# Layer 0's attention with the two query halves in the two row halves of TensorE's array

## The chip, the cores and the metric

The kernel runs on one core of a Trainium2 chip. The metric is the device time of one execution in microseconds (us). The engines are TensorE (PE; its weight loads are shown as PEld), VectorE (DVE), ScalarE (ACT), GpSimd (POOL) and SyncE (SP, which issues the DMAs). The numbers are float32; most matmuls read their operands as fp32r, those of the probabilities with the values as plain f32.

## The reference, cut to what matters

Two layers follow each other over 1024 latent tokens and 256 context tokens. Layer 0 is grouped-query attention with 16 heads of 64 numbers and 4 groups, layer 1 latent attention with 16 heads. The change is in layer 0's attention:

```python
def gqa_attend(q, k, v):
    s = jnp.einsum('bqhgd,bkhd->bhgqk', q, k).astype(jnp.float32) * (GQA_HEAD_DIM ** -0.5)
    p = jax.nn.softmax(s, axis=-1).astype(v.dtype)
    return jnp.einsum('bhgqk,bkhd->bqhgd', p, v)
```

Latent queries read all 1280 keys, context queries the 256 context keys. Queries and keys are normed and rotated before.

## The kernel before, in words

**Order of the work.** Layer 0's projections come first (to about 275 us of the profile), then gate slices for layer 0 (`gate_slice`, to 368 us; the first row maxima stand among them), layer 0's attention (368 to 765 us), its output projection with layer 1's projections, layer 1's attention (1197 to 1642 us) and the last output projection.

**Split numbers.** Every query and key is kept as a rounded number and a rest (QH and QL, KH and KL), since an fp32r product rounds its operands. A score is KH·QH + KL·QH + KH·QL, less a shift, which is the largest product of the query's row. Layer 0 has heads of 64 numbers, so before the change a tile KA holds KH in rows 0 to 63 and KL in rows 64 to 127, QA holds QH twice, KB holds KH with a row of -1 below it (65 rows), and QB holds QL with the row of shifts `crow` below it. KA·QA and KB·QB are then all of it, in two steps (`l0_scores`, L1141).

**Units.** The class `Attention` works through units. A latent unit is one head with its 1024 queries and ten tiles of 128 keys; a context unit is one group's four heads with 256 queries each and two key tiles. There are 16 latent and 4 context units in layer 0. For each key tile `do_scores` (L413) issues two steps for each of the two query halves of 512 (four matmuls at L422) into a score tile `st` of two PSUM banks, of which there are two, and ACT makes the probabilities `p` of it (L424). After the unit's tiles, `do_av` (L458) multiplies the probabilities by the values: the outputs of the two query halves lie in PSUM partitions 0 to 63 and 64 to 127, each step 128 rows by 64 columns.

**Maxima.** The row maxima of units to come are made between the score steps: a matmul of 128 queries by 512 keys into a PSUM tile `mx` (L362; for the context keys two of 256, L367), which DVE then reduces (L363, L369). A latent unit needs 20 of them, a context unit 4; `do_scores` puts two into each key tile, in front of the first and of the third matmul, and `maxima` lets them run 28 ahead. There are two `mx` buffers. When a unit's maxima are there, DVE takes the largest (L376), PE turns them (L382, "turn"), DVE copies (L384) and a DMA writes the row `crow`.

**Sums.** POOL adds up the first six probability tiles (L445), DVE the last four in pairs (L431). One unit later PE folds the sum over the partitions with four 32-column steps (`total`, L500), into the old `av` tile; DVE transposes it and takes reciprocals (L504, L505). Then POOL scales the output (L519, L520).

**What sets the order.** In `run` the orders of PE, DVE and ACT are written out by hand (`manual_schedule`): the unit's key tiles, the turn, the total of the unit before, then `do_av`. In the gate slices before 368 us a scheduler places the maxima, four after each gate slice (L1171 and on, `at.maxima(at.done + 4, 2)`). POOL's and SP's orders are the scheduler's everywhere.

## Time and profile before

| what | value |
|---|---|
| time, median of 3 runs (lowest, highest) | 1738.92 us (1737.24, 1739.38) |
| profiled execution, first to last instruction | 1736.6 us |
| layer 0's attention in it | 368 to 765 us |
| granted TensorE clock, mean | 0.997 |
| HBM read and written | 158.98 and 73.63 MB |

The profiled execution is told by its span; the three timed runs lie 0.6 to 2.8 us above that span, with what lies around the instructions. A row of the timeline gives the start, the time to the end of the last instruction of the row, engine, line, names, and the number of merged instructions. A matmul's own duration contains a latency, so the pace is read from the distance of two starts. PEld is the load of the stationary operand that belongs to each matmul.

### The profile page before, as it was taken

The page shows a single profiled execution, that of the slowest core. Times are in us where ns is not written, and L with a number is a line of the kernel's source. Part 1 is how long each engine was busy: PE and PEld are TensorE (multiplying, and loading weights), DVE is VectorE, ACT ScalarE, POOL GpSimd, SP SyncE. Part 2 cuts the span into 40 slices and gives each one's busy share as a digit, 9 for nine tenths or more (in the row PEclk, how much of TensorE's full clock was granted, in tenths as well). Part 3 has the DMA queues.
Part 4 walks back from the last instruction along what each step waited for, and adds up shares of the span by engine and source line. Part 5 has one row for each costly group of instructions (what it writes and reads, how often), then busy time and mean ns, then how long its engine had stood idle before and what let it go on. Part 6 is the DMA issues. An engine that isn't in the chain of part 4 may idle for free. (4 is left out here: it accounts for less than half of the span.)

```text
span 1736.6 us, 23794 instructions
## 1 busy us (share of the span) xinstructions
PE 1703.1 (98%) x8548; PEld 1232.5 (71%) x8548; DVE 1068.4 (62%) x1807; ACT 644.5 (37%) x943; POOL 979.5 (56%) x657
## 2 busy tenths in 40 slices
PE   8999999999999999999989999999999999999998
PEld 5776778776655665558878798978666666657587
DVE  3765651368777877625575667756676767667231
ACT  4632221134544544433244633332343443434310
POOL 2763430237888897752344644443587878777511
PEclk9999999999999999999999999999999999999999
DMA  9457854432332422156434857685434443441452
GB/s 326 156 160 235 265 167 136 133 98 55 100 91 71 116 66 74 44 145 189 137 94 132 238 163 199 181 234 162 104 88 118 108 104 91 111 112 43 118 162 73
DMA packets 211901, 234.33 MB, mean 135 GB/s; under 512 B 20680, under 2 KB 157880, under 8 KB 211784
## 3 DMA queue, kind: packets, MB, share of 16 engines
q1 hardware_dynamic: 211360, 232.71, 47.2%
q8 instruction: 67, 1.10, 0.3%
q14 instruction: 50, 0.41, 0.1%
q10 hardware_dynamic: 424, 0.11, 0.0%
HBM read 158.98 MB, written 73.63 MB: 134 GB/s over the span
## 5 line engine op out<-in xcount | busy, mean ns | idle before, releaser
L363 DVE TENSOR_REDUCE m<-mx 128x1 f32<-128x512 f32 x512 | 351.5, 691 | 203.6 <-PE mx L362 201.5
L424 ACT ACTIVATE p<-st 128x1024 f32<-128x1024 f32 x328 | 335.3, 1024 | 219.5 <-PE st L422 185.1
L445 POOL TENSOR_TENSOR acp<-acp,p 128x1024 f32<-128x1024 f32 x128 | 305.7, 2388 | 8.7
L458 PE MATMUL av<-p,v 128*64 128x512 f32 x1312 | 289.9, 595 | 0.0
L458 PEld LDWEIGHTS av<-p,v 128*64 128x64 f32 x1312 | 90.8, 137 | 181.0 <-issue 178.6
L445 POOL TENSOR_TENSOR acp<-p 128x1024 f32<-128x1024 f32 x34 | 81.3, 2391 | 168.3 <-ACT p L424 167.9
L445 POOL TENSOR_TENSOR acp<-acp,acd 128x1024 f32<-128x1024 f32 x60 | 141.5, 2358 | 22.2 <-DVE acd L431 19.4
L431 DVE TENSOR_REDUCE acd<-p 128x512 f32<-128x1024 f32 x124 | 144.6, 1219 | 7.7 <-ACT p L424 7.7
L135 POOL TENSOR_TENSOR wb<-wraw,wa 128x512 fp32r<-128x512 f32 (+3 forms) x73 | 95.5, 1324 | 90.6 <-ACT wa L156 90.0
L92 PE MATMUL mm<-wa,hh 128*128 128x512 f32 (+2 forms) x336 | 127.3, 379 | 1.7 <-ACT hh L787 1.7
L422 PE MATMUL st<-QH,KL 96*128 96x512 f32 x320 | 123.5, 392 | 0.0
L94 PE MATMUL mm<-wa,hl 128*128 128x512 f32 (+2 forms) x336 | 121.3, 361 | 1.4 <-DVE hl L790 1.4
L93 PE MATMUL mm<-wb,hh 128*128 128x512 f32 (+2 forms) x336 | 120.9, 360 | 0.0
L479 ACT COPY os<-av 128x512 f32<-128x512 f32 x36 | 21.1, 586 | 252.9 <-PE av L458 173.5
L369 DVE TENSOR_REDUCE m<-mx 128x2 f32<-128x512 f32 x144 | 99.3, 692 | 25.3 <-PE mx L367 24.4
L92 PE MATMUL y<-wa,oh 128*128 128x512 f32 (+1 forms) x296 | 114.1, 386 | 0.0
L93 PE MATMUL y<-wb,oh 128*128 128x512 f32 (+1 forms) x296 | 113.6, 384 | 0.0
L94 PE MATMUL y<-wa,ol 128*128 128x512 f32 (+1 forms) x296 | 113.6, 384 | 0.0
L422 PE MATMUL st<-QA,KA 128*128 128x512 f32 x336 | 106.6, 399 | 0.7 <-ACT p L424 0.7
L422 PE MATMUL st<-QB,KB 65*128 65x512 f32 x336 | 105.5, 395 | 0.0
L362 PE MATMUL mx<-KA,QA 128*128 128x512 f32 x256 | 102.4, 405 | 1.2 <-DVE m L363 1.0
L362 PE MATMUL mx<-KH,QH 96*128 96x512 f32 x256 | 102.3, 401 | 0.0
(232 smaller groups left out, 3423.4 us busy)
## 6 DMA issues: line engine op xcount, KB each, us to landing
mraw<-in_l_w_mod SPq DMA_DIRECT2D x64, 256.0 KB
wraw<-in_l_w_in SPq DMA_DIRECT2D x28, 512.0 KB
rb<-rrow SPq DMA_DIRECT2D x72, 128.0 KB
mraw<-in_l_w_mod SPq DMA_DIRECT2D x16, 512.0 KB
sgd<-gth SPq DMA_DIRECT2D x32, 256.0 KB
QA<-q0h SPq DMA_DIRECT2D x32, 256.0 KB
wraw<-in_l_w_out SPq DMA_DIRECT2D x16, 512.0 KB
sg<-sgd SPq DMA_DIRECT2D x64, 128.0 KB
```

The source lines that it names most:

```text
L92: pe.matmul(ps, lhsT=lh(k), rhs=rh(k), start=first and i == 0, stop=False)
L93: pe.matmul(ps, lhsT=lh(k), rhs=rl(k), start=False, stop=False)
L94: pe.matmul(ps, lhsT=ll(k), rhs=rh(k), start=False, stop=last and i == len(ks) - 1)
L135: eng.tensor_sub(lo, a, b)
L362: pe.matmul(m, lhsT=s["mq"][:, i * P:(i + 1) * P], rhs=s["mk"][:, n * 512:(n + 1) * 512], start=True, stop=True)
L363: dve.reduce_max(s["m"][:, i, n:n + 1], m, axis=AX.X)
L369: dve.reduce_max(s["m"][:, 2 * i:2 * i + 2, 2 if u["kind"] == "lat" else 0], m.rearrange("p (a b) -> p a b", a=2), axis=AX.X)
L422: pe.matmul(ps[:, n * 512:(n + 1) * 512], lhsT=lh, rhs=rf(n), start=(j == 0), stop=(j == len(prods) - 1))
L424: act.activation(p, ps, AF.Exp, scale=self.ops["scale"])
L431: dve.reduce_sum(t[:, ns], p2.rearrange("p a n -> p n a")[:, ns, :], axis=AX.X)
L445: pool.tensor_add(t, a, b)
L458: pe.matmul(s["av"][64 * n:64 * n + 64, :], lhsT=s["v"][:, kt, u["vc"]:u["vc"] + 64], rhs=p[:, n * 512:(n + 1) * 512], start=kt == kts[0], ...
```

## The change

In layer 0 alone (`HALVES = (True, False)`; the functions for layer 1 are there, but not called) each query half gets its own 64 rows of the array: QH and QL are tiles of 128 rows by 512, with the first query half in rows 0 to 63 and the second in rows 64 to 127; KA holds KH in both row halves, KB holds KL in both. A score is then four steps of 64 rows for each half: KH·QH, KL·QH, KH·QL, and a step that subtracts the shift, in which the stationary tile `minus` has -1 in rows 0 and 64 and a tile `shift` the shifts in the same rows (zeros elsewhere, written once). `scores_by_halves` writes the steps of the two halves alternately. A maximum is one product of 64 rows with KH and QH alone; two are made per key tile, one in each row half, the second put after two of the other half's steps. The `mx` tiles go from two to three, the `av` tiles from two to one, and the total goes to an `mx` tile. The row of shifts is written by two DMAs in place of one, from one buffer in place of two. The diff, cut to layer 0:

```diff
+HALVES = (True, False)
...
-            self.ps_m = st.enter_context(tc.tile_pool(name=f"psm{l}", bufs=2, space=PSUM, side="right", reuse_waits="tile"))
+            self.ps_m = st.enter_context(tc.tile_pool(name=f"psm{l}", bufs=3 if HALVES[l] else 2, space=PSUM, side="right", reuse_waits="tile"))
+            if HALVES[l]:
+                self.ops["open"](self, st)
...
-                setattr(self, name, stp.enter_context(tc.tile_pool(name=f"{name}{l}", bufs=2, space=PSUM, reuse_waits="tile")))
+                bufs = 1 if HALVES[l] and name == "ps_o" else 2
+                setattr(self, name, stp.enter_context(tc.tile_pool(name=f"{name}{l}", bufs=bufs, space=PSUM, reuse_waits="tile")))
...
+        def max_parts(self, u, step):
+
+            s = self.state[id(u)]
+            kind, i, n = step
+            if kind == "lat":
+                half, spans = i // 4, [(i % 4, slice(n * 512, n * 512 + 512), slice(0, 512))]
+            else:
+                half, spans = i // 2, [(2 * (i % 2) + a, slice(NL, NT), slice(a * 256, a * 256 + 256)) for a in range(2)]
+            held = {}
...
+            def part(j):
+                if j == 0:
+                    held["m"] = self.ps_m.tile([P, 512], F32, name="mx", tag="mx")
+                pairs = self.ops["maxima"](s, half)
+                q, k = pairs[j]
+                for t, ks, cs in spans:
+                    pe.matmul(held["m"][:, cs], lhsT=q[:, t * P:(t + 1) * P], rhs=k[:, ks], start=j == 0, stop=j == len(pairs) - 1)
+                if j == len(pairs) - 1:
+                    dve.reduce_max(s["m"][:, i, n:n + 1], held["m"], axis=AX.X)
...
-                r = self.sm.tile([8, P], F32R, name="crow", tag="crow", bufs=2)
+                r = self.sm.tile([8, P], F32R, name="crow", tag="crow", bufs=1)
                 dve.tensor_copy(r, t)
-                sp.dma_start(raw(s["crow"]), raw(r))
+                if HALVES[self.l]:
+                    for n in range(2):
+                        sp.dma_start(raw(s["crow"][n]), raw(r[4 * n:4 * n + 4, :]))
+                else:
+                    sp.dma_start(raw(s["crow"]), raw(r))
...
+            if HALVES[self.l]:
+                if lat:
+                    self.todo += [(u, ("lat", i + 4 * a, n)) for i in range(4) for n in range(2) for a in range(2)]
+                self.todo += [(u, ("ctx", i + 2 * a, 0)) for i in range(2) for a in range(2)]
...
+        @staticmethod
+        def side_by_side(*streams):
+
+            for t in range(max(map(len, streams))):
+                for stream in streams:
+                    if t < len(stream):
+                        stream[t]()
...
+        def scores_by_halves(self, u, kt, p, steps):
+
+            s = self.state[id(u)]
+            ps = self.ps_s.tile([P, 1024], F32, name="st", tag="st")
+            prods = [self.ops["scores"](s, kt, n) for n in range(2)]
+            last = len(prods[0]) - 1
...
+            streams = [[lambda j=j, n=n: product(j, n) for j in range(last + 1)] for n in range(2)]
+            for half, parts in steps:
+                at_ = (last + 2) // 2 if half else 0
+                streams[half][at_:at_] = parts
+            self.side_by_side(*streams)
+            act.activation(p, ps, AF.Exp, scale=self.ops["scale"])
...
-                t = s["av"] if u is not self.units[-1] else self.ps_m.tile([P, 512], F32, name="mx", tag="mx")
+                t = s["av"] if u is not self.units[-1] and not HALVES[l] else self.ps_m.tile([P, 512], F32, name="mx", tag="mx")
...
-                            self.do_scores(u, kt, ps[i], one_more)
+                            if HALVES[self.l]:
+                                count += 2
+                                self.scores_by_halves(u, kt, ps[i], self.next_maxima(count, t + 1 + ahead))
+                            else:
+                                self.do_scores(u, kt, ps[i], one_more)
...
+    def l0_open(at, st):
+        pool_ = st.enter_context(tc.tile_pool(name="shift0", bufs=1, **right))
+        at.minus = pool_.tile([P, P], F32R, name="minus")
+        at.shift = [pool_.tile([P, 512], F32R, name=f"shift{i}") for i in range(4)]
+        for t in (at.minus, *at.shift):
+            pool.memset(raw(t), 0.0)
+        for n in range(2):
+            pool.memset(raw(at.minus[64 * n:64 * n + 1, :]), -1.0)
...
-            KB = kp.tile([65, NT], F32R, name="KB", tag="KB")
...
+            KB = kp.tile([P if HALVES[0] else 65, NT], F32R, name="KB", tag="KB")
+            if HALVES[0]:
+                for t, src in ((KA, k0h), (KB, k0l)):
+                    for n in range(2):
+                        sp.dma_start(raw(t[64 * n:64 * n + 64, :]), src[g // 2, r, :])
...
+    def l0_maxima(s, n):
+        r = slice(64 * n, 64 * n + 64)
+        return [(s["QH"][r, :], s["KH"][r, :])]
+
+    def l0_scores(s, kt, n=None):
         ks = slice(kt * P, (kt + 1) * P)
+        if n is not None:
+            r = slice(64 * n, 64 * n + 64)
+            return [(s["KH"][r, ks], s["QH"][r, :]), (s["KL"][r, ks], s["QH"][r, :]),
+                    (s["KH"][r, ks], s["QL"][r, :]), (s["minus"][r, :], s["X"][r, :])]
```

Two places of TensorE's order show what moves. The first is the end of a latent unit's scores in layer 0 (its last key tile, then turn, total and the products with the values), before the change; `mx` are maxima, `st` scores, `av` outputs, `acp` the sum of the unit before:

```order
L362 MATMUL mx<-KA,QA 128x512
L422 MATMUL st<-QA,KA 128x512 x2
L362 MATMUL mx<-KA,QA 128x512
L422 MATMUL st<-QB,KB 128x512 x2
L382 MATMUL mx<-ident,m_3747 8x128
L500 MATMUL av<-acp,twos 32x256 x4
L458 MATMUL av<-p,v 64x512 x20
```

The same place after the change, where each `x2` of a score is one step in each row half (`shift_2949` is the unit's tile of shifts):

```order
L393 MATMUL mx<-KA,QH 128x512
L501 MATMUL st<-QH,KA 128x512 x2
L501 MATMUL st<-QH,KB 128x512 x2
L393 MATMUL mx<-KA,QH 128x512
L501 MATMUL st<-QL,KA 128x512 x2
L501 MATMUL st<-shift_2949,minus 128x512 x2
L422 MATMUL mx<-ident,m_3829 8x128
L597 MATMUL mx<-acp,twos 32x256 x4
L555 MATMUL av<-p,v 64x512 x20
```

Six matmuls of a key tile have become ten, five in each row half; turn, total and the products with the values stand where they stood, and the total's target is now an `mx` tile.

The second place is in the gate slices ahead of the attention (`mm` are gate products), before the change, the four maxima behind one slice:

```order
L362 MATMUL mx<-KA,QA 128x512 x2
L92 MATMUL mm<-hh,wa 128x512
L93 MATMUL mm<-hl,wa 128x512
L94 MATMUL mm<-hh,wb 128x512
L362 MATMUL mx<-KA,QA 128x512
L92 MATMUL mm<-hh,wa 128x512
L93 MATMUL mm<-hl,wa 128x512
L94 MATMUL mm<-hh,wb 128x512
L92 MATMUL mm<-hh,wa 128x512
L93 MATMUL mm<-hl,wa 128x512
L362 MATMUL mx<-KA,QA 128x512
```

And after it:

```order
L95 MATMUL mm<-hh,wb 128x512
L393 MATMUL mx<-KA,QH 128x512 x3
L93 MATMUL mm<-hh,wa 128x512
L94 MATMUL mm<-hl,wa 128x512
L393 MATMUL mx<-KA,QH 128x512
L95 MATMUL mm<-hh,wb 128x512
```

The third maximum has moved up to the first two (the second of them stands in the other row half), and the fourth stands alone, two gate products later.

128 lines of the change are left out of this document (116 added, 12 removed).

## The prediction

> **What bounds the kernel now.** I read the page first, then a table of stretches, then TensorE's timeline through one unit of layer 0's attention, since the change is there alone. The page's line of busy times:
>
> ```profile
> PE 1703.1 (98%) x8548; PEld 1232.5 (71%) x8548; DVE 1068.4 (62%) x1807; ACT 644.5 (37%) x943; POOL 979.5 (56%) x657
> ```
>
> TensorE is hardly ever idle, so the question is what it is busy with, and what comes next if it needs less. The timeline of PE over one latent unit (start, length, instruction, merged count):
>
> ```profile
> 389.25 0.60 PE L458 MATMUL av<-p,v 128*64 128x512 f32 x2
> 389.78 0.50 PE L362 MATMUL mx<-KA,QA 128*128 128x512 f32 x1
> ...
> 402.47 0.40 PE L362 MATMUL mx<-KA,QA 128*128 128x512 f32 x1
> ...
> 403.41 0.62 PE L422 MATMUL st<-QB,KB 65*128 65x512 f32 x2
> 403.87 0.27 PE L382 MATMUL mx<-ident,m 128*8 128x128 f32 x1
> 404.07 0.64 PE L500 MATMUL av<-acp,twos 128*32 128x256 f32 x8
> 404.64 8.80 PE L458 MATMUL av<-p,v 128*64 128x512 f32 x40
> 413.37 0.50 PE L362 MATMUL mx<-KA,QA 128*128 128x512 f32 x1
> 413.71 0.63 PE L422 MATMUL st<-QA,KA 128*128 128x512 f32 x2
> ```
>
> A key tile is 402.47 to 403.87 = 1.40 us for six matmuls, so 0.233 us a step. Ten tiles take 389.78 to 403.87 = 14.09 us, turn and total 0.77, the products with the values 8.73: 23.59 us a unit. The engines in the score stretch and in the stretch of the values (columns: length, then PE, PEld, DVE, ACT, POOL, clock, DMA):
>
> ```profile
> 390.00:404.00 14.00, 14.00 (x65) 11.21 (x64) 13.52 (x21) 9.71 (x10) 9.70 (x5) 1.00 0.00 0
> 404.60:413.30 8.70, 8.70 (x44) 2.79 (x40) 5.06 (x6) 0.49 (x1) 6.38 (x3) 1.00 0.43 107
> ```
>
> In the score stretch DVE is busy 13.52 of 14.00 us, almost as long as PE. A shorter stretch must therefore show that DVE can go faster. The groups from 381 to 709 us give durations and counts (name, shape, count, busy, mean ns):
>
> ```profile
> L363 DVE TENSOR_REDUCE m<-mx 128x1 f32<-128x512 f32 x209 | 143.3, 690 | 59.1 <-PE mx L362 58.0
> L458 PE MATMUL av<-p,v 128*64 128x512 f32 x576 | 127.1, 595 | 0.0
> L367 PE MATMUL mx<-KA,QA 128*128 128x256 f32 x120 | 24.0, 282 | 0.0
> L367 PEld LDWEIGHTS mx<-KA,QA 128*128 128x128 f32 x120 | 22.5, 188 | 5.5 <-DVE m L369 0.3
> L382 PE MATMUL mx<-ident,m 128*8 128x128 f32 x16 | 4.4, 274 | 0.4 <-DVE m L363 0.4
> ```
>
> The 576 products with values are 14 latent units of 40 and two context units of 8.
>
> **Do two halves run side by side?** No row halves are in this trace, but column halves are: the row at 389.25 has two matmuls in 0.60 us although one takes 0.595 (L458), so they run together. They write different PSUM partitions; row halves write the same partitions of different banks, which no row shows. I take it that a pair of row halves costs one step of 0.233. Nearest rows: the values' 40 steps in 8.73 us give 0.218 as lower end. For the upper end, the weight loads: each pair needs two. A load takes 188 ns, but two matmuls of 256 columns (L367, next fence, the row at 372.43: 0.41 for two of 0.282) start 0.13 apart, each with a load of its own, so a load holds its path 0.13 us at most. Two in a row would make a pair 0.26; the later start of the first hides some of it, and I take 0.25.
>
> **The score stretch after.** TensorE needs five pairs a tile, 5 x 0.233 = 1.16 us. Two other loops set a floor. The first is the score buffer. The attention's first tiles have no maxima, and PE waits there for ACT (PE's rows and then one of ACT; the row at 380.84 ends the unit):
>
> ```profile
> 369.06 0.74 PE L422 MATMUL st<-QA,KA 128*128 128x512 f32 x2
> ...
> 371.39 0.73 PE L422 MATMUL st<-QA,KA 128*128 128x512 f32 x2
> ...
> 372.43 0.41 PE L367 MATMUL mx<-KA,QA 128*128 128x256 f32 x2
> ...
> 380.84 0.27 PE L382 MATMUL mx<-ident,m 128*8 128x128 f32 x1
> ```
>
> ```profile
> 369.10 1.03 ACT L424 ACTIVATE p<-st 128x1024 f32<-128x1024 f32 x1 [0.55 <-PE st L422]
> ```
>
> From a tile's first product (369.06) to that of the tile which reuses its buffer (371.39) it is 2.33 us: four steps, the wait for the last result, 1.03 us of ACT and the release. After the change the first score product stands in the first pair of a tile and the last in the fifth, one step more: 2.33 + 0.23 = 2.56 for two tiles, 1.28 a tile. The second loop is DVE, whose reductions take 0.69 us but overlap when two are waiting:
>
> ```profile
> 398.84 0.68 DVE L363 TENSOR_REDUCE m<-mx 128x1 f32<-128x512 f32 x1
> ...
> 399.43 0.68 DVE L363 TENSOR_REDUCE m<-mx 128x1 f32<-128x512 f32 x1
> ```
>
> 399.43 - 398.84 = 0.59, so two maxima need 1.2 us a tile if the third `mx` buffer keeps DVE fed. The score buffer's 1.28 is the longest. The first two tiles find both buffers free: tile 9 starts at 4 x 2.56 + 1.16 = 11.40 and ends at 12.56. The first load of the stretch stays bare (413.71 - 413.37 = 0.34 in place of 0.233: 0.11), and the context maxima put two 256-column products into one half while the other waits, and the entry for the unit's largest value shifts one step; I take 0.2 of the 0.3 to 0.5 this makes, since part falls into ACT's wait. 12.87 against 14.09: **1.2 us for each of 14 units, 16.8**.
>
> The first unit has six tiles with maxima in 380.84 - 372.43 = 8.41, 1.40 each: 6 x 0.12 = 0.7. Two context units have maxima; both buffers are free in their two tiles, which go from 1.40 to 1.16:
>
> ```profile
> 461.02 0.50 PE L362 MATMUL mx<-KA,QA 128*128 128x512 f32 x1
> ...
> 464.01 0.64 PE L500 MATMUL av<-acp,twos 128*32 128x256 f32 x8
> ...
> 745.49 0.73 PE L422 MATMUL st<-QA,KA 128*128 128x512 f32 x2
> ...
> 749.93 3.65 PE L458 MATMUL av<-p,v 128*64 128x512 f32 x16
> ```
>
> Four tiles at 0.24: 0.9. The tiles without maxima (745.49 to 749.93, four in 4.44) still have four steps between first and last product: nothing. **Saved in the attention: 18.4.**
>
> **What it costs.** Changes of the array's shape. A turn of 0.27 us (403.87) is followed 0.20 later by the four column strips of the total, while a 0.28 us product is followed 0.13 later by one of its own shape: about 0.08 lost, and 0.11 more where a 128-column load is then bare. I price a change at 0.2, with zero as other end. One is new at each turn, from row halves to the whole array; the 16 turns stand in 14 places: +2.8. In the gate slices, four changes come with each group of four maxima:
>
> ```profile
> L362 PE MATMUL mx<-KA,QA 128*128 128x512 f32 x32 | 12.3, 424 | 1.2 <-DVE m L363 1.0 <-DMA KA<-k0l 0.2
> ```
>
> 32 latent maxima and four of context keys are nine groups. Before, a group is 4 x 0.233 = 0.93; after, the three take two steps, the lone one a third: 0.70 + 4 x 0.2 = 1.50. 9 x 0.57 = +5.1, and with free changes 9 x -0.23 = -2.1.
>
> The Trainium skill (TensorEngine Tiling (Array Packing), Key Properties) says that a change of the tiling mode, not of the tile alone, drains TensorE; it gives no figure. The 0.20 behind the turn agrees. Without that rule the changes would be free and the sum -20.5, so 1718.
>
> At no cost: the total in an `mx` buffer (DVE has finished its maxima about when PE has its last step, and has 8.7 us of the values' stretch, of which it uses 5.06, to clear it), one `av` buffer (ACT copies it before the next unit's scores end), the second crow DMA (nine us ahead of its reader), and POOL, which gets fewer writes of constants; its 9.70 + 6.38 = 16.1 busy us in these two stretches, with some 3 more for scaling, stay under the new 22.4 of a unit.
>
> **Sum**: -18.4 + 2.8 + 5.1 = -10.5 on a span of 1736.6: 1726.1. The median of the runs is 2.3 above the span, so 1738.92 - 10.5 = **1728.4**. With 0.218 a pair (loop 2.50, stretch 12.4; 14 x 1.7 + 2.1 = 25.9) and free changes it is -28.4: 1710.5. With 0.25 (loop 2.63, stretch 13.3: 14 x 0.8 + 1.0 = 12.2) it is -4.3: 1734.6.
>
> **Rivals.**
>
> DVE becomes the bound. For it: 13.52 of 14.00 busy, and 0.69 is the common duration; the overlap of 0.59 is seen only where two were waiting. At 0.69 the last maximum waits for the reduction three before it, 0.54 + 17 x 0.69 + 0.06 = 12.3, three more steps end at 13.0, and the total waits for a free buffer until 13.7: some 0.55 a unit saved, 14 x 0.55 = 7.7 against 7.9 of changes: 1739, no change. Against it stands the third buffer.
>
> Slower: the row halves do not run side by side, and the change doesn't do what it says. Place: every pair of L501. A pair then costs 0.465, a tile 2.33, +0.93 on 150 tiles with maxima, and 1.86 for 1.11 on 18 without: 139.5 + 13.5 + 7.9 = +161, 1900. It decides from the distance of two pairs' starts: above 0.264 (50 steps x 0.264 + 0.3 = 13.5) the gain no longer pays the 7.9. Against it are the column halves; for it, that no row shows two halves writing the same partitions.
>
> Milder, of the same sign: a half's next weights cannot load beneath its own matmul. PEld is busy 11.21 us beneath a PE busy all 14.00, so with the whole array they can. Were it otherwise in halves, a pair costs the 0.34 of the row at 413.37: 150 x 0.30 + 18 x 0.25 + 7.9 = +57, 1796. The Trainium skill (TensorE: Matmul & The Clock Gate, Part 3, The mechanism) says in its list of what overlaps that loads overlap running matmuls only in another row group, which would give this time; this case's trace, with loads beneath matmuls of the same 128 rows, speaks against it.
>
> **How the numbers follow.** Forecast, 1710 to 1735: 0.66. More than that (free changes and a quicker buffer loop): 0.05. DVE as bound, 1735 to 1742: 0.15. Serial halves 0.10, bare loads 0.04. Range 1708 to 1742; it leaves out the last two. About 0.2% (3.5 us, 1735.4 to 1742.4) is what a measurement can tell. Faster: 0.66 + 0.05 = 0.71. Same: 0.12 of the third case. Slower: its other 0.03 and the last two, 0.17.
>
> **What would show it.** In the profile after: pairs of score steps whose rows start together and follow each other after 0.22 to 0.25; score stretches of a unit of about 12.9 in place of 14.09; PE waiting for ACT's p at a tile's start; DVE reductions 0.6 apart; each group of gate maxima about 0.5 longer. Wrong would be: score stretches near 13.5 with PE waiting for DVE, pairs 0.34 or more apart, or turns that start without a loss.

## The result and the profile after

| | time, us (lowest to highest) | ratio to the kernel before, 95% interval |
|---|---|---|
| before | 1738.47 (1737.24 to 1739.38), 4 runs | |
| after | 1727.68 (1726.59 to 1731.57), 4 runs | 0.9943 [0.9928, 0.9957] |
| predicted | 1728.4 (1708 to 1742) | |

The kernel became 10.8 us faster. The profiled execution of after is the slowest of its four: 1731.57 us, with a span of 1729.8. Its line of busy times:

```profile
PE 1693.6 (98%) x9220; PEld 1206.9 (70%) x9220; DVE 1048.5 (61%) x1807; ACT 645.2 (37%) x943; POOL 977.9 (57%) x660
```

TensorE is as full as before. To see where the time went I cut every profile at three places: where TensorE starts the first product of the last twelve gate slices, where it starts the first score (`st`), and where it starts the first product of the next stage (`y`). The lengths in us, for this and for all the experiments below:

| profile | ahead of the gate slices | gate slices | attention of layer 0 | behind it |
|---|---|---|---|---|
| before | 301.4 | 66.5 | 396.9 | 971.8 |
| after | 305.3 | 69.5 | 379.3 | 975.7 |
| c_after (after, again) | 304.5 | 68.9 | 380.4 | 972.9 |
| e1_front | 302.0 | 69.6 | 374.8 | 974.8 |
| e2_two_mx | 302.9 | 73.4 | 392.3 | 971.9 |
| e3_serial | 303.7 | 68.9 | 388.6 | 975.0 |
| e4_one_half | 302.6 | 68.9 | 509.0 | 970.2 |
| e5_late_total | 302.1 | 71.8 | 377.5 | 974.3 |
| e6_gate5 | 302.5 | 62.9 | 384.5 | 972.3 |
| e7_all_three | 305.0 | 65.7 | 381.4 | 971.8 |
| e8_short_max | 302.4 | 68.8 | 373.6 | 972.0 |
| e9_act_queue | 302.9 | 68.9 | 377.5 | 972.8 |
| e10_gate7 | 303.0 | 66.1 | 379.8 | 975.1 |
| e11_best | 302.4 | 66.1 | 376.2 | 972.1 |

The attention lost 16.5 to 17.5 us and the gate slices took 2.3 to 3.0 us more. The first and the last column belong to stages that no kernel here changes; they scatter by 3.3 and by 5.5 us between the executions with the change. Part of this is TensorE's clock: outside the gate slices, the attention and the last instructions the granted clock was 0.50 for 6.8 us in before, for 20.5 in after (6.8 of them from 26.8 us on) and for 13.7 in c_after. So the two middle columns are what to compare, and a difference of a few us between two spans says little by itself.

One latent unit on TensorE after the change (start, length, instruction, merged count):

```profile
395.93 0.50 PE L393 MATMUL mx<-KA,QH 64*128 64x512 f32 x1
395.93 0.73 PE L501 MATMUL st<-QH,KA 64*128 64x512 f32 x2
...
398.56 0.50 PE L501 MATMUL st<-QH,KA 64*128 64x512 f32 x2
...
400.05 0.39 PE L501 MATMUL st<-QH,KB 64*128 64x512 f32 x2
400.28 0.39 PE L393 MATMUL mx<-KA,QH 64*128 64x512 f32 x1
...
401.16 0.50 PE L501 MATMUL st<-QH,KA 64*128 64x512 f32 x2
```

```profile
408.85 0.27 PE L422 MATMUL mx<-ident,m 128*8 128x128 f32 x1
409.05 0.64 PE L597 MATMUL mx<-acp,twos 128*32 128x256 f32 x8
...
418.35 0.50 PE L393 MATMUL mx<-KA,QH 64*128 64x512 f32 x1
```

Three things are to be seen. The two matmuls of a pair are one row, x2, in the 0.39 us of one, and the next pair follows 0.23 later (400.05 to 400.28). The scores of ten tiles take 395.93 to 408.85 = 12.92 us. Eleven of the fourteen units take 12.91 to 12.96, where before had 14.06 to 14.19; the other three take 13.05, 13.08 and 13.37, where before had 14.56, 14.69 and 14.81, and in these the turn came 0.71 us after the last score step, waiting for VectorE, and now comes 0.43 after it. In sum the fourteen fell by 17.3 us. And the unit's period is 418.35 - 395.93 = 22.42 us in place of 23.59. The stretch of the scores, in the columns of before:

```profile
396.00:408.40 12.40, 12.35 (x103) 9.29 (x104) 11.67 (x20) 9.34 (x10) 8.53 (x4) 1.00 0.01 1
```

DVE is busy 11.67 of 12.40 us, hardly less dense than before. What stands behind TensorE's next step is told by the waits of its weight loads over the whole attention (us in total, times, longest):

```profile
PEld st L501 <- ACT p L508: 22.5, 67, 0.7
```

67 times a tile's first load waits for ScalarE's exponential of the tile that held the buffer: it is the score buffer's loop. Between the first products of two tiles that share a buffer lie 401.16 - 398.56 = 2.60 us; 2.56 was forecast.

### The profile page after: what moved, and what is told of

Same layout as the page of the kernel before. It is cut to its first block, busy times and chain, and to the rows that moved or that the text cites. A ratio compares the mean times of both kernels' runs of the same rounds, so it can differ in the third digit from the quotient of the medians.

```text
span 1729.8 us, 25188 instructions
## 1 busy us (share of the span) xinstructions
PE 1693.6 (98%) x9220; PEld 1206.9 (70%) x9220; DVE 1048.5 (61%) x1807; ACT 645.2 (37%) x943; POOL 977.9 (57%) x660
## 5 line engine op out<-in xcount | busy, mean ns | idle before, releaser
L369 DVE TENSOR_REDUCE m<-mx 128x1 f32<-128x512 f32 x256 | 176.8, 691 | 123.7 <-PE mx L368 123.1
L395 DVE TENSOR_REDUCE m<-mx 128x1 f32<-128x512 f32 x256 | 159.8, 683 | 80.3 <-PE mx L393 78.7
L93 PE MATMUL mm<-hh,wa 128*128 128x512 f32 x256 | 101.7, 397 | 0.0
L95 PE MATMUL mm<-hh,wb 128*128 128x512 f32 x256 | 101.0, 395 | 0.0
```

The costliest lines, as they stand in the source:

```text
L93: pe.matmul(ps, lhsT=lh(k), rhs=rh(k), start=first and i == 0, stop=False)
L95: pe.matmul(ps, lhsT=ll(k), rhs=rh(k), start=False, stop=last and i == len(ks) - 1)
L369: dve.reduce_max(s["m"][:, i, n:n + 1], m, axis=AX.X)
L395: dve.reduce_max(s["m"][:, i, n:n + 1], held["m"], axis=AX.X)
```

## The experiments

My theory at this point: pairs of row halves share one step, the pace of a tile is the score buffer's loop, a change of the array's shape costs about 0.2 us where a bare load comes with it. The rivals: VectorE sets the pace; the side by side is worth less than it looks; the gate's price is something else.

### c_after: the changed kernel again

No edit, five timings.

> The changed kernel once more, unchanged, timed in more rounds and with a second profile. In the first profile 3.5 us were lost before the first row maximum (319.1 in place of 315.6 us) and 3.9 us behind the attention, where the change touches nothing. Theory A, these stages vary from one execution to the next: first maximum again within 1.5 us of 315.6, and the stages behind the attention within 2 us of those of before; span 1723 to 1727. Theory B, the change causes them (other addresses, other DMA order): again 319 us and a span near 1730. Both expect score stretches of 12.9 us and a time of 1726 to 1729 us.

Measured: 1727.37 us (1726.15 to 1730.27), ratio 0.9935 [0.9921, 0.9949]. The span is 3.2 us below that of the first profile; the two stages that nothing here touches are 3.6 us shorter (304.5 for 305.3, 972.9 for 975.7); the gate slices and the attention together differ by 0.4. The span is the one of theory A, and so are the stages behind the attention, but the first maximum stands at 318.3 us, between the two theories. The clock fits this: half of the time at 0.50, an estimate of what it cost, is 10.2 us in the two outer columns of the first profile, 6.8 in c_after and 3.4 in before. Without it these columns are 1270.7, 1270.6 and 1269.8 us together, and 1267.7 to 1274.7 in all the executions with the change. So beside the clock no cost of the change shows there. Whether the change makes the clock fall more often stays open: the mean granted clock is 0.9971 in 38 timed executions of before and 0.9962 in the nine of the changed kernel, by estimate 1.6 us.

The attention of c_after has one stretch of 14.11 us, which the first profile lacks. TensorE waits there for the row of shifts:

```profile
492.27 0.68 PE L501 MATMUL st<-shift,minus 64*128 64x512 f32 x2 [0.73 <-DMA shift<-crow]
```

It is the second latent stretch behind the first context unit, and the place comes back in the experiments below.

### e1_front: both maxima in front of a tile's scores

```diff
-                at_ = (last + 2) // 2 if half else 0
+                at_ = 0
```

> Both maxima of a key tile stand as one pair in front of its score products, where before the second stood behind two products of its half. First and last score product are then four steps apart in place of five. Theory A, the two score buffers set the pace of the changed kernel (2.56 us for two tiles): the loop shrinks by one step to 2.33, the floor becomes VectorE's two reductions of 0.60 us, a score stretch goes from 12.94 to 12.2 to 12.5 us, and the time falls by 6 to 10 us to some 1719. Theory B, VectorE and the supply of its buffers set the pace: two maxima at the same time give it no more room, stretches stay at 12.9 us or grow, time 1727 to 1735. Theory C, TensorE's own five steps set it: no change, 12.9 us and 1727.

Measured: 1724.12 us (1722.97 to 1725.94), ratio 0.9916 [0.9903, 0.9930]. Eleven stretches are 12.41 to 12.47 us and three 12.52 to 12.88, as expected. The same row of waits as above, in this kernel, with one that is new:

```profile
PEld mx L597 <- POOL acp L542: 4.1, 2, 2.2
...
PEld st L501 <- ACT p L508: 3.2, 7, 0.7
```

The wait for ScalarE falls from 22.5 us to 3.2. So the loop of the score buffer was the bound, and the maximum in the middle of a tile made it one step longer. The time fell by 3.3 us and not by the expected 6 to 10: fourteen stretches at 0.5 are 7, of which the attention shows 4.5 to 5.6. What was given back stands in the two context units, where the total now waits for GpSimd's sum. Of after, the first of them:

```profile
463.60 0.50 PE L393 MATMUL mx<-KA,QH 64*128 64x512 f32 x1
...
466.92 0.64 PE L597 MATMUL mx<-acp,twos 128*32 128x256 f32 x8 [0.77 <-POOL acp L542]
```

and of e1_front:

```profile
458.75 0.50 PE L393 MATMUL mx<-KA,QH 64*128 64x512 f32 x2
...
462.88 0.64 PE L597 MATMUL mx<-acp,twos 128*32 128x256 f32 x8 [1.45 <-POOL acp L542]
```

From the unit's first product to the total it is 3.33 us in after and 4.14 in e1_front; in the second context unit 2.53 and 4.48.

### e2_two_mx: the third buffer taken back

```diff
-bufs=3 if HALVES[l] else 2, space=PSUM, side="right"
+bufs=2, space=PSUM, side="right"
```

> Two buffers for the maxima in place of three, all else as changed. Theory A (score buffers set the pace, the third maxima buffer keeps VectorE from becoming the bound): with two, a maximum waits for the reduction two before it, matmul to release is 0.44 + 0.69 + 0.06 = 1.2 us, so stretches grow by about 0.4 us and the total waits for a buffer at the unit's end: 12.94 to 13.3 or 13.6 us, plus 0.2 to 0.4 us ahead of the total; time 1733 to 1742, the gain mostly gone. Theory B, the third buffer is worth nothing because TensorE's steps set the pace: 12.9 us, 1727.

Measured: 1742.78 us (1740.08 to 1747.22), ratio 1.0022 [1.0011, 1.0034]. Most stretches are 13.2 us and the gate slices take 4 us more. Behind a unit's scores the total has no free buffer:

```profile
411.02 0.27 PE L422 MATMUL mx<-ident,m 128*8 128x128 f32 x1
411.50 0.64 PE L597 MATMUL mx<-acp,twos 128*32 128x256 f32 x8 [0.20 <-DVE m L395]
```

and the maxima wait for VectorE's reductions:

```profile
PEld mx L393 <- DVE m L395: 14.0, 70, 0.3
```

Turn to total is 0.48 us here and 0.20 in after. The third `mx` buffer is worth 15 us: without it the change makes the kernel 0.2% slower. With two buffers it is thus as in the prediction's rival in which VectorE decides, which was priced at 1739.

### e3_serial: the two halves written one behind the other

```diff
-            self.side_by_side(*streams)
+            self.side_by_side(streams[0] + streams[1])
```

> The same matmuls, but the five steps of the first query half stand in the order ahead of the five of the second, so that only the last of the first half can run beside the first of the second. Theory A, the gain comes from two row halves running side by side: a tile then takes about 8 steps of 0.23 us, 1.85 us in place of 1.28, stretches grow to 18 to 19 us and the time to some 1805 to 1820. Theory B, the gain comes from fewer rows or shorter products and not from pairs: stretches of about 13 us, time below 1740.

Measured: 1737.98 us, one run. My expectation was wrong: stretches of 13.4 us and not 18 to 19. What stands in the program for TensorE in one tile (number, line, instruction):

```
1486 L501 MATMUL st<-QH,KA 128x512
1487 L501 MATMUL st<-QH,KB 128x512
1488 L501 MATMUL st<-QL,KA 128x512
1489 L501 MATMUL st<-shift_2948,minus 128x512
1490 L501 MATMUL st<-QH,KA 128x512
1491 L501 MATMUL st<-QH,KB 128x512
```

and what TensorE did with such a tile:

```profile
396.88 0.51 PE L501 MATMUL st<-QH,KA 64*128 64x512 f32 x2
397.22 0.40 PE L501 MATMUL st<-QH,KB 64*128 64x512 f32 x2
397.45 0.39 PE L501 MATMUL st<-QL,KA 64*128 64x512 f32 x1
397.47 0.39 PE L393 MATMUL mx<-KA,QH 64*128 64x512 f32 x1
```

The two products QH,KA are four places apart in the program and stand in one row (they start 13 ns apart). TensorE itself brings products of different row halves together over some places of its queue. The careful order of the diff is therefore worth 8.3 to 8.7 us in the two middle columns (10.6 between one run and a median), and not the whole of the side by side.

### e4_one_half: both query halves in the same row half

```diff
-            r = slice(64 * n, 64 * n + 64)
+            r = slice(0, 64)
             return [(s["KH"][r, ks], s["QH"][r, :]), (s["KL"][r, ks], s["QH"][r, :]),
```

> The changed kernel with the scores of both query halves taken from rows 0 to 63 (for the second half too the operands of the first are read, so the scores of the second half of the queries are those of the first half's operands); the maxima stay one in each half. Theory A, that the gain comes from two products of different row halves sharing one step of 0.2275 us: the eight products of a tile now follow one another in one half, 8 x 0.2275 = 1.82 us, and the maximum of the same half makes it up to 2.05 us a tile where the changed kernel shows 1.29. A score stretch takes 18.5 to 20.8 us in place of 12.94, sixteen units and four short ones make 85 to 120 us more: 1812 to 1848 us. Rival B, that ScalarE's exponential and VectorE's maxima set the pace of a tile and the side by side is hidden behind them: the stretch stays under 13.5 us and the time within 1725 to 1735 us.

Measured: 1852.43 us, one run. From the start of a tile's scores:

```profile
400.56 0.39 PE L501 MATMUL st<-QH,KA 64*128 64x512 f32 x1
...
401.02 0.62 PE L501 MATMUL st<-QH,KB 64*128 64x512 f32 x2
401.49 0.62 PE L501 MATMUL st<-QL,KA 64*128 64x512 f32 x2
```

Now a pair takes 0.62 us and the next follows 0.46 later, two steps. A stretch is 20.7 us, at the upper end of the 18.5 to 20.8 expected, and the time 4 us over the upper end of the range; of the 129 us more in the attention some 11 lie in the last tiles, which have no maxima. The side by side itself is worth 1852 - 1727 = 125 us in this layout. It pays only 10.8 against before because the layout has ten products of 64 rows in a tile where before had six of up to 128: side by side they are five steps for six, and singly nine.

### e5_late_total: e1_front, and in two context units the total behind the values

```diff
+                        held = []
+                        if not whole and not late:
+                            held, self.totals = self.totals, []
                         while self.totals:
                             self.totals.pop(0)()
...
                         self.do_av(u, group, ps)
+                        for f in held:
+                            f()
```

> The kernel with both maxima in front (e1_front, 1724.1 us), and in the two middle context units the total of the unit before moved behind that unit's own products with the values. Theory A, that the gain which e1_front fell short of was given back because TensorE waits there for GpSimd's sum: the two context stretches took 4.14 and 4.48 us in e1_front and 3.33 and 2.53 in the changed kernel, so the wait of 1.5 to 2 us in each goes, 2.5 to 3.5 us in all, and the time is 1721 us (1720 to 1722.5). Rival B, that the wait only moves (the total waits for GpSimd behind the products as well, or the next unit's first scores do): 1723.5 to 1725 us.

Measured: 1727.48 us (1725.18 to 1729.85), ratio 0.9933 [0.9921, 0.9946]: 3.4 us slower than e1_front. Up to the first step of the products with the values the two context units take 2.65 and 2.63 us. The total itself now stands behind; from a context unit's first product to the next unit's it is 1.2 and 1.5 us less than in e1_front, 2.7 together, as theory A says. But the second latent stretch behind the first of them takes 17.36 us in place of 12.43:

```profile
492.86 0.97 PE L501 MATMUL st<-shift,minus 64*128 64x512 f32 x2 [3.10 <-DMA shift<-crow]
```

The shift row is late, for a reason that lies on SyncE's queue. In e1_front (start, length, line, transfer):

```profile
470.81 0.58 SPq L603 DMA_DIRECT2D rrow<-cr  x1
...
479.60 1.10 SPq L621 DMA_DIRECT2D od<-os  x2
...
483.98 1.33 SPq L427 DMA_DIRECT2D shift<-crow  x2
```

and in e5_late_total:

```profile
474.83 0.53 SPq L603 DMA_DIRECT2D rrow<-cr  x1
...
485.90 1.10 SPq L621 DMA_DIRECT2D od<-os  x2
...
489.66 1.33 SPq L427 DMA_DIRECT2D shift<-crow  x2
```

This execution was late before the attention already: its first context unit starts at 461.04 us and that of e1_front at 458.75, 2.3 us earlier. Against the start of that unit the total is 0.7 us later, its reciprocals leave 1.7 later, GpSimd scales later, the store that waits for GpSimd is 4.0 late on the queue, and the row behind it 3.4, while TensorE comes to the unit that needs the row 1.0 us earlier. The wait moved off TensorE and came back through two engines and a queue.

The 2 to 3 us more in the gate slices are two things: 1.1 us is a wait for a transfer at the first maxima, and right behind it, from 318.92 us on, the granted clock is 0.50 for 3.4 us, which makes eight steps 0.2 us longer each:

```profile
317.54 0.49 PE L393 MATMUL mx<-KA,QH 64*128 64x512 f32 x2 [1.12 <-DMA sgd<-gth]
```

### e6_gate5: five gate groups in place of nine

```diff
-                if (m or s0 == 1024) and (m, s0) != (3, 1024):
+                if (m, s0) in ((1, 1024), (2, 0), (2, 512), (2, 1024), (3, 0)):
                     at.maxima(at.done + 4, 2)
+                if (m, s0) == (3, 512):
+                    at.start_unit()
...
-    at.run(28, 3, pieces, lambda: first.extend(fetch_first(0, 2)))
+    at.run(24, 3, pieces, lambda: first.extend(fetch_first(0, 2)))
```

> The changed kernel with maxima in five gate groups in place of nine; the second unit's twenty maxima move into the tiles of the first unit, the lead is 24 and no longer 28. Theory A, that a gate group with four maxima costs 1.49 us, half of it the change of the array's shape and the bare loads around: four groups less are 4 x 1.49 = 6.0 us less, and the sixteen maxima make eight pairs more in the tiles, at 0.23 to 0.3 us each 1.8 to 2.4 us more; the time falls by 3.6 to 4.2 us from 1727.5 to 1723.5 us (1722 to 1725). Rival B, that the maxima cost in a gate group no more than their steps (two pairs of 0.2275, 0.46 us a group): 1.8 us less and 1.8 to 2.4 more, no change (1727 to 1728.5).

Measured: 1724.18 us (1723.53 to 1726.54), ratio 0.9920 [0.9906, 0.9933]. The time is the expected one, but by luck: the gate slices lose 6.0 to 6.6 us against the two profiles of the changed kernel (6.0 expected; 1.57 a group in the mean), the attention takes 4.1 to 5.2 more (1.8 to 2.4 expected), and together they gain only 1.4 to 1.9 us. The rest of the 3.3 us lies in the stages that no kernel here changes. The first stretch must make up for the missing maxima and meets VectorE's pace, and two turns come before their maxima are done:

```profile
366.65 0.49 PE L393 MATMUL mx<-KA,QH 64*128 64x512 f32 x1 [0.32 <-DVE m L395]
```

```profile
448.35 0.27 PE L422 MATMUL mx<-ident,m 128*8 128x128 f32 x1 [0.65 <-DVE m L416]
```

### e7_all_three: the three edits together

> Maxima in front, late totals in the context units and five gate groups together. Theory A, that the three terms lie at different places and add: 1727.5 - 3.3 - 3 - 4 = 1717 us (1715 to 1719.5). Rival B, that VectorE, whose two reductions a tile take 1.2 us where the loop with both maxima in front takes 1.245, gives part of it back when eight more pairs come into the tiles: 1720 to 1723 us.

Measured: 1725.66 us (1721.87 to 1728.63), ratio 0.9920 [0.9907, 0.9933], not 1717. The reason is neither theory's: the gate slices are short and the context stretches 2.63 and 2.65, but the stall of e5_late_total is here too (one stretch of 17.57 us), and so are the waits for VectorE of e6_gate5 (2.9 us together).

### e8_short_max: VectorE relieved

e1_front, with reductions half as wide:

```diff
-                    dve.reduce_max(s["m"][:, i, n:n + 1], held["m"], axis=AX.X)
+                    dve.reduce_max(s["m"][:, i, n:n + 1], held["m"][:, :256], axis=AX.X)
```

and `scale=0.001` for 0.125.

> The kernel with both maxima in front (e1_front, 1724.1 us, latent score stretches of 12.43 us), and VectorE's reductions of the latent maxima over the first 256 keys of each 512 only, with the exponential's scale at 0.001 (so the maxima of the other keys are left out, and the probabilities are others). Theory A, that with the buffers' loop out of the way VectorE's two reductions a tile, 2 x 0.60 = 1.20 us, set the pace of 1.245 us: they fall to some 0.35 us each, and TensorE's five steps, 5 x 0.2275 = 1.14 us, set it; a stretch takes 11.4 to 11.8 us, fourteen times 0.6 to 1.0 us less, and the time is 1710 to 1716 us. Rival B, that ScalarE's exponential (1.03 us and its way there and back) still sets it: the stretch stays at 12.3 to 12.5 us and the time at 1722 to 1726 us.

Measured: 1718.52 us, one run. Ten stretches are 12.06 to 12.12 us, where e1_front has 12.43, and four are 12.38 to 12.81: between both theories. VectorE's group and ScalarE's rows in one stretch:

```profile
L395 DVE TENSOR_REDUCE m<-mx 128x1 f32<-128x256 f32 x16 | 6.0, 419 | 6.7 <-PE mx L393 6.7
```

```profile
398.17 2.19 ACT L508 ACTIVATE p<-st 128x1024 f32<-128x1024 f32 x2 [0.24 <-PE st L501]
400.58 2.13 ACT L508 ACTIVATE p<-st 128x1024 f32<-128x1024 f32 x2 [0.22 <-PE st L501]
```

VectorE now stands idle 6.7 us of the stretch until the maxima come, so in e1_front it was the bound, by some 0.35 us a stretch. Behind it the buffers' loop appears again: two exponentials follow two others after 2.41 us, 2.1 of which ScalarE is busy. Three loops lie within 0.1 us of each other per tile: VectorE at 1.24, ScalarE with the buffers at 1.20, TensorE at 1.14 (an estimate, five steps of 0.2275; no run shows a tile at that pace).

The attention as a whole is only 1.2 us shorter than in e1_front, since the granted clock fell to 0.50 for 3.4 us behind each of the two waits for GpSimd's sum. The first of them, and the stretch behind it in the columns of before:

```profile
461.57 0.64 PE L597 MATMUL mx<-acp,twos 128*32 128x256 f32 x8 [1.98 <-POOL acp L542]
```

```profile
462.25:465.66 3.41, 3.41 (x8) 0.61 (x8) 0.67 (x2) 0.00 (x0) 1.24 (x1) 0.50 0.21 79
```

Behind the waits of 1.45 and 1.77 us at the same places of e1_front the clock stayed at 1.00. The time of this one run is thus, by estimate, 3.4 us longer than the reductions alone would make it.

### e9_act_queue: e5_late_total, the shift row issued by ScalarE

```diff
-                        sp.dma_start(raw(s["crow"][n]), raw(r[4 * n:4 * n + 4, :]))
+                        act.dma_start(raw(s["crow"][n]), raw(r[4 * n:4 * n + 4, :]))
```

> e5_late_total (1727.5 us) with the two transfers of the shift row issued by ScalarE and no longer by SyncE. In e5_late_total both context stretches fell as expected, to 2.65 us, but one latent stretch took 17.36 us in place of 12.43: the shift row's transfer was issued 5.7 us later than in e1_front (489.66 against 483.98), behind a store on SyncE's queue that waits for GpSimd. Theory A, that this queue is the whole of it: without it the stretch is 12.4 to 12.6 us again, 4.9 us go, and the time is 1722 us (1720.5 to 1723.5), 2 us under e1_front. Rival B, that the row's other way (VectorE's copy, ScalarE's own work, the transfer itself) is as late: the stretch stays over 15 us and the time over 1725 us.

Measured: 1725.90 us (1723.90 to 1728.76), ratio 0.9932 [0.9918, 0.9946]. Theory A fails: the stretch is still 17.50 us. ScalarE had nothing before it on its queue, VectorE's copy was there at 477.51, and still:

```profile
484.42 3.29 ACTq L427 DMA_DIRECT2D shift<-crow  x2
```

The two issues stand at 484.42 and 487.13. In the program the first waits, beside VectorE, for the semaphore DMAHW6 and the second for DMAHW0; the transfers take eight such semaphores in turn, so each waits for the older transfer that has its semaphore to land. The trace's marks of the landings say which these are. The first waits for a load of KB (320 KB), issued by SyncE at 479.33 and landed at 484.35. The second waits for the second half of the output's store, issued by SyncE at 484.72, behind the first half, which waits for GpSimd; it landed at 487.11. And then the row's second half, 2 KB, took until 490.74, while the DMA engines were busy all the time. So moving the row to another engine takes it past SyncE's queue, but not past the store that waits for GpSimd, which holds its semaphore.

The stall is 3.3 us long (from 487.46 to 490.78) but costs 5. Two stretches of time behind it (length, PE, PEld, DVE, ACT, POOL, granted clock, DMA):

```profile
490.70:491.70 1.00, 0.92 (x4) 0.89 (x6) 0.01 (x1) 0.03 (x1) 0.92 (x2) 0.50 0.76 141
491.70:492.70 1.00, 1.00 (x7) 0.92 (x7) 1.00 (x2) 0.99 (x1) 1.00 (x1) 0.50 0.00 0
```

The granted clock is 0.50 from 490.58 to 493.99, 3.4 us, and a pair takes 0.42 there: about eight pairs lose 0.2 us each.

### e10_gate7: e9_act_queue with seven gate groups

```diff
-                if (m or s0 == 1024) and (m, s0) != (3, 1024):
+                if (m > 1 or (m and s0)) and (m, s0) != (3, 1024):
```

> e9_act_queue with maxima in seven gate groups in place of nine and the lead as in the changed kernel. e6_gate5 showed 6.3 us less in the gate stage for four groups, 1.57 us a group, and 4.6 us more in the attention, since its first stretch had twenty-six maxima to do in ten tiles and VectorE takes 0.6 us for one, and since its turns came before their last maxima were there. Theory A: with seven groups the first stretch has its even two maxima a tile from the first tile, 2 x 1.57 = 3.1 us go in the gate stage, 0.2 to 0.4 us come in the first stretch, and no turn is early: 2.8 us under e9_act_queue, 1719 us (1717 to 1721). Rival B, that the gate stage's gain is given back in the attention as in e6_gate5: within 1 us of e9_act_queue.

Measured: 1724.22 us (1723.23 to 1725.89), ratio 0.9919 [0.9906, 0.9933], 1.7 us under e9_act_queue and outside both theories. The gate slices lose 2.7 us (3.1 expected). The attention takes 2.3 more, 2.0 of it in the one stalled stretch (19.46 us for 17.50), 0.4 elsewhere, as expected. So the gate's term is confirmed, and the late row eats most of it.

### e11_best: both maxima in front, seven gate groups, the late total in the second context unit alone

```diff
-                        if not whole and not late:
+                        if not whole and not late and t > 4:
```

(against e5_late_total; the gate as in e10_gate7, the row on SyncE).

> Both maxima in front (e1_front), seven gate groups with maxima (e10_gate7), and the total behind the products in the second context unit alone; at the first one the order of e1_front stays, and the shift row stays on SyncE. Theory A, that the stall of 5 us behind the first context unit comes from the total there being later (its reciprocals' transfer 4 us later, and with it GpSimd's scaling, the store on SyncE that waits for it, the loads and the shift row), and that the three terms lie apart otherwise: from the stages of e1_front, 69.6 us of gate stage become 66.1, the second context stretch 4.48 becomes 2.63 with 0.15 given back in the next, the first stretch takes 0.35 more, no stretch is over 13 us but the first: gate and attention together 444.4 - 3.5 - 1.7 + 0.35 = 439.6 us, and the time is 1719.5 us (1717.5 to 1721.5). Rival B, that the shift row of one stretch comes late here too: a stretch of 15 us or more, and 1722 to 1726 us.

Measured: 1718.58 us (1718.34 to 1721.42), ratio 0.9883 [0.9866, 0.9899]. This beats both kernels: 20 us under before, 9 under after. The gate slices take 66.1 us, the second context stretch 2.63. Gate and attention are 442.3 and not 439.6, since two short waits for the shift row are left, one in the second latent stretch behind each context unit:

```profile
486.28 0.77 PE L501 MATMUL st<-shift,minus 64*128 64x512 f32 x2 [0.60 <-DMA shift<-crow]
```

```profile
581.29 0.68 PE L501 MATMUL st<-shift,minus 64*128 64x512 f32 x2 [0.90 <-DMA shift<-crow]
```

Their stretches are 13.49 and 13.68 us, most others 12.4 to 12.6. With these two at 12.45 the sum would be 440.0.

## Why the prediction was right

**A pair is one step: right.** Pairs follow one another after 0.227 to 0.235 us (0.233 taken), the two starts of a pair 3 to 4 ns apart. e4_one_half shows the other case of the prediction at its place, two steps a pair and 1852 us (1900 priced). The milder rival, that a half's next weights can't load beneath its own matmul, is gone with the same rows: a pair with two loads of 0.18 us each in every 0.23 us leaves no room for bare loads. The rule of the Trainium skill that the prediction named there (TensorE: Matmul & The Clock Gate, Part 3, The mechanism) would have made 1796; the trace disagrees with it.

**The score buffer's loop sets the pace: right.** 2.60 us for two tiles against 2.56; most stretches 12.91 to 12.96 against 12.87, of which 0.09 is the turn's change of shape that I had priced apart. 14 x (14.09 - 12.94) = 16.1 us saved at the usual stretch and 17.3 in sum, with the turn's 0.09 in it; 16.8 was forecast without. e1_front takes the one extra step out of the loop and the wait falls from 22.5 to 3.2 us, which shows it.

**VectorE can go faster than its 0.69 us: right, with a buffer's help.** With eight reductions in a row it is:

```profile
404.17 5.06 DVE L395 TENSOR_REDUCE m<-mx 128x1 f32<-128x512 f32 x8
```

(5.06 - 0.68) / 7 = 0.63 us apart; 0.60 was taken. e2_two_mx and e8_short_max show how near this bound lies.

**The first unit: right,** 12.25 us in place of 12.88 from the first score to the turn, 0.63 (0.7). **The context units: wrong.** 0.9 was forecast, and it is 0.1: 2.99 became 2.53 in one, and 3.33 in the other, where the total waits 0.77 us for GpSimd. The step that failed is the line "at no cost ... POOL": I had weighed GpSimd's busy time against a latent unit's period and not against the place where its sum is due: behind a latent unit stand only the two tiles of the context unit, 2.5 us, before the total needs it.

**The row of shifts at no cost: wrong behind the context units.** The same line had its second transfer nine us ahead of its reader. That holds behind latent units, but behind the first context unit before had only 2.6 us already, since the row stands there in SyncE's queue behind the store that waits for GpSimd:

```profile
488.45 0.70 SPq L385 DMA_DIRECT2D QB<-crow  x1
```

```profile
491.08 0.62 PE L422 MATMUL st<-QB,KB 65*128 65x512 f32 x2
```

The change makes two transfers of it, and TensorE comes to the place earlier: in c_after it waits 0.73 us, in the first profile not. In e3_serial, e5_late_total to e7_all_three and e9_act_queue to e11_best it waits 0.4 to 4.1 us at this place.

**The change of shape: right in the gate, half as dear at a turn.** Rows of after around a group of maxima:

```profile
326.18 0.39 PE L94 MATMUL mm<-hl,wa 128*128 128x512 f32 x1
326.41 0.39 PE L95 MATMUL mm<-hh,wb 128*128 128x512 f32 x1
326.73 0.73 PE L393 MATMUL mx<-KA,QH 64*128 64x512 f32 x3
327.38 0.50 PE L93 MATMUL mm<-hh,wa 128*128 128x512 f32 x1
327.72 0.40 PE L94 MATMUL mm<-hl,wa 128*128 128x512 f32 x1
```

From a product to the first maximum it is 0.32 us, 0.09 over the 0.23 between two products; the second product after the maxima comes 0.34 after the first, 0.11 over, since its load is bare. Together 0.20, as priced. A group is three steps, four changes and four bare loads: 3 x 0.2275 + 4 x 0.095 + 4 x 0.108 = 1.49 us, 1.57 by e6_gate5 and 1.37 by e10_gate7; 1.50 was forecast. At a turn no 128-column load is bare, and only the 0.09 stays: 14 x 0.09 = 1.3 in place of 2.8. The turn waiting for VectorE isn't the reason: from the last score step to the turn it is 0.31 to 0.33 us at the usual turn of after, and just so in e8_short_max and e4_one_half, where VectorE's last reduction ended as little as 0.06 us or as much as 0.27 before the turn; before had 0.23. The drain that the Trainium skill states (TensorEngine Tiling (Array Packing), Key Properties) is this 0.09, as far as these rows can tell it from the loads.

**The gate stage: right after, too cheap before.** The stage's own products are 192 x 0.2275 + 96 x 0.12 = 55.2 us. The stage as a whole, in before and in after:

```profile
301.43:367.97 66.54, 65.35 (x332) 54.22 (x330) 30.12 (x50) 10.46 (x20) 12.42 (x10) 1.00 0.35 108
```

```profile
305.25:374.75 69.50, 69.10 (x333) 51.65 (x331) 29.36 (x50) 10.46 (x20) 10.04 (x8) 1.00 0.40 117
```

So the maxima cost 14.3 us after (13.7 in c_after; 13.5 forecast) and 11.3 before, where I had 8.4. Of those 2.9, 1.2 are the waits for VectorE and for keys that the prediction's row of L362 ended with and its sum left out; 1.0 more is one late step in each of the nine groups, where the product behind a maximum comes 0.11 late in before too, by the size of a bare load; the last 0.7 I didn't trace. The term is +2.3 to +3.0 and not +5.1.

**The sum.** Forecast -10.5: attention -15.6 with the turns, gate +5.1. Measured: attention -16.5 to -17.5, gate +2.3 to +3.0, together -14.2 to -14.6. The medians show -10.8. The difference lies in the outer columns, which the sum took as fixed: together 1273.2 us in the one profile of before, whose span is that of its median run, and 1280.9 and 1277.4 in the two of the changed kernel. About 1.6 us of it is the lower granted clock of the timed runs, by the estimate under c_after; the rest is less than these columns scatter, so whether the change costs anything there stays open. The forecast of 1728.4 is thus nearer to 1727.7 than its terms are, and that is luck: the attention came out 0.9 to 1.9 us better and the gate 2.1 to 2.8, and the outer stages, of which the forecast said nothing, gave 3 to 4 us back.

## What to carry to other kernels

When several loops lie close together (here VectorE, the buffers' loop and TensorE within 0.1 us a tile), a saved step shows only up to the next loop, so count each loop's length from the first use of a buffer to its next, with everything that stands between first and last write; here, moving a maximum from the middle of a tile to its front was worth more than its cost in work. A wait that is taken off one engine has to be followed through every queue behind it: the total 0.7 us later made a store 4.0 late, and with it a small row that TensorE needed 24 us on. Moving such a row to another queue doesn't help where it takes its turn on a semaphore with larger transfers (e9_act_queue). And price a stage by its stage: GpSimd had room over a unit and none in the two tiles where its sum was due.

## What the runs showed of the hardware

- TensorE brings matmuls of different row halves together although they stand four places apart in its program (e3_serial: 13.4 us a stretch with all of one half written before the other, 20.7 in e4_one_half where they can't meet).
- The granted clock fell to 0.50, for 3.4 us each time, at the end of a wait of 2.9 us (e9_act_queue, pairs after 0.42 us in place of 0.23), and also soon behind waits of 1.1 us (e5_late_total, from 318.9 us on) and of 2.0 and 1.8 us (e8_short_max). Behind the 0.77 us in after's context unit and the 1.45 and 1.77 us of e1_front it stayed at 1.00. So a wait of between one and two us may or may not cost another 1.7 us (an estimate, half of 3.4), and its length alone doesn't tell. The Trainium skill (TensorE: Matmul & The Clock Gate, Part 1, What's actually happening) gives about 3.4 us for both the idle window and the way back; the way back agrees, and the waits before the fall were shorter than such a window.
- A transfer of 2 KB on an otherwise empty queue (ScalarE's) was issued 7 us after its data were there (484.42 against 477.51), since the program has it wait for the semaphore of an older transfer of 320 KB, which landed at 484.35. Its other half, issued at 487.13, took 3.6 us to land, with the DMA engines busy all the time.
